# Neighbourhood attention: exponentials copied by a DMA into tiles of the rounded type, and transposed as that type

## The chip, the cores and the metric

The kernel runs on one core of a Trainium2 chip. The metric is the device time of one execution in microseconds (us), as the median of several runs; before the change it is 2466.07 us, from three runs between 2465.53 and 2466.47. PE is the matrix engine, PEld its weight loads, DVE the vector engine, ACT the scalar engine, POOL the third elementwise engine, and SP the engine that issues the kernel's DMAs.

## The reference

One layer of an encoder is applied to two sequences of 2048 tokens with 1024 columns each, all in 32-bit floats. Two attentions run beside each other on one input projection, and their outputs go into one product:

```python
def encoder_layer(x, p, ...):
    h = rms_norm(x, norm_w)
    proj = h @ w_in                       # 3328 columns
    q_a, k_a, v_a, g_a, q_b, k_b, v_b, g_b = jnp.split(proj, IN_SPLITS, axis=-1)
    ...
    o_a = windowed_gqa_sink(q_a, k_a, v_a, sink_a) * jax.nn.silu(g_a)
    ...
    o_b = neighbourhood_attn(q_b, k_b, v_b, rpb_b) * jax.nn.silu(g_b)
    x = x + jnp.concatenate([o_a, o_b], axis=-1) @ w_out
    gate = jax.nn.sigmoid(x @ w_ple_gate)
    return x + (p @ w_ple) * gate
```

The change is in the second attention, `neighbourhood_attn`. The tokens lie on a grid of 32 rows and 64 columns; each of 8 heads (64 columns a head) looks from a token at a window of 8 rows and 16 columns of the grid:

```python
sc = jnp.einsum('bnqhd,banchd->bnhqac', qr, kb) * scale
sc = jnp.where(mask, sc + bias, -jnp.inf)
pr = jax.nn.softmax(sc, axis=-1)
o = jnp.einsum('bnhqac,banchd->bnqhd', pr, vb)
```

## The kernel before

**Precision.** A matrix product is taken in `F32R`, a 32-bit type that PE multiplies with fewer bits than `F32`. To keep the accuracy, an operand is split into two `F32R` parts: high, the value as rounded when it is written as `F32R`, and low, the remainder. A product then takes three matmuls (high with high, low with high, high with low), or two where one side is laid out so that both of its parts stand beside each other. The parts are made by ACT (high) and DVE or POOL (low). Transposes were made in `F32` by PE: `tr` (L254) with the tile to be turned and an identity, `ident` (L111) or `rowwise` (L114), an identity with its columns in another order.

**Stages.** Up to about 804 us stage A works on the first attention, 32 blocks of tokens in two units each. From 804 to 1813 us stage B works on the second attention: 64 units `unit_b` (L845), one for a block of 8 x 16 queries and four of the eight heads. Then come the output product and the last product with its gate (from L1122 on). The products of a unit stand between those of a stream of projections (`proj_b`, L758, writing `pqk` and `pvg`) and later of `p @ w_ple` (`ple_ahead`), so that PE has products to do while the other engines work on the unit.

**One unit of stage B.** For each of four heads: `sc` makes the scores in `scb` (two matmuls), and `softmax` (L264) on DVE adds the bias and takes the maximum into a tile `s` (tag `s`, 5 buffers). After the fourth head `exps` (L275) makes the negated maxima `nm`, and ACT makes four exponentials, each in place in `s` (L284), and their sums. They are written in the order of heads 0, 2, 1, 3, and only the first is held in the program's order (`P`, L286). Then `load_values` (L862) loads the values in chunks, `vw`, three or four loads of up to 256 KB each (L870). For each head in that same order, `pt` turns three or four chunks of the exponentials (some 96 to 128 columns each) with `rowwise` into `ptb` (L255), ACT writes the high part and DVE the low part into `p_t`, and `po` multiplies them with `vw` into `pob`. `fin` scales with the gate and stores the block with a DMA to `ob_d` (L928).

**What sets the order.** `PLAN_B` (L94) gives the share of the unit's length at which each of these steps is written: scores from 0.00 to 0.11, exponentials and value loads at 0.16, the four groups of transposes at 0.45, 0.52, 0.60 and 0.74, with the steps named by `now` = 0 belonging to the unit before. Every matmul and transpose is pinned behind the one before it (`pinned`, L237), so PE's order is that of the program. On the other engines a scheduler orders the instructions by when it holds them to be ready, but for those under `P` or `behind`. SP issues all the DMAs that matter here, in one order, and waits with an instruction until all that it needs is done; what stands behind it waits too.

**The start.** `make_identity` and the copy to `rowwise` are POOL's. The first loads on SP are those of the first tokens (`stx`) with slices of the weights (`ws`, L232), then the second tokens, more weights (`ws`, `wg`) and small tables (`rw`, `snk_all`). The first products `pk` (keys and values of the first two blocks of tokens) and `pq` wait for them.

**Tiles by tag.** `ev` has 3 buffers: in stage A it holds pairs of score tiles (`s2`), in stage B from `ple_ahead` on the evictions `ev`. In between, in stage B, it has no other use.

Of the kernel before, what the change touches and what calls it, by code (L numbers as in the profile page):

```python
# [11 lines left out]
F32 = mybir.dt.float32  # L12
F32R = mybir.dt.float32r
# [55 lines left out]
SB = 5  # L69
# [11 lines left out]
TAIL = 8100  # L81
HOLD = {"wa": 20, "wb": 12, "wp": 0}
TW = 512
NU = SEQ // TW
AHEAD = 5
CP = 2
# [14 lines left out]
def emit(ctx, tc, io):  # L101
    nc = tc.nc
    dram = ctx.enter_context(tc.tile_pool(name="dram", bufs=1, space=bass.MemoryType.DRAM))
    cp = ctx.enter_context(tc.tile_pool(name="const", bufs=1))
# [3 lines left out]
        tag = PSM.get(tag, tag)  # L108
        return pp.tile(shape, F32, tag=tag, name=name, bufs=PSB[tag])

    ident = cp.tile([128, 128], F32, tag="ident", name="ident")  # L111
    make_identity(nc, ident)

    rowwise = cp.tile([128, 128], F32, tag="rowwise", name="rowwise")  # L114
    nc.gpsimd.tensor_copy(rowwise.rearrange("p (r c) -> p r c", c=16), ident.rearrange("p (c r) -> p r c", r=8))
    nw = cp.tile([128, KT], F32, tag="nw", name="nw")
    nc.scalar.dma_start(nw, io["norm_w"])
    ms_a = cp.tile([128, 2 * NT], F32, tag="ms_a", name="ms_a")
# [8 lines left out]
    main = ctx.enter_context(tc.tile_pool(name="main", bufs=1))  # L127
# [109 lines left out]
    def pinned(ins):  # L237

        if last_pe:
            tc.add_manual_dep(ins.ins, last_pe.pop().name,  # L240
                              mybir.DependencyInfo(mybir.DependencyClass.NoSync, mybir.DependencyReason.DATA),
                              reason="tensor engine order")
        last_pe.append(ins.ins)

    def behind(ins, other=None):

        tc.add_manual_dep(ins.ins, (other or last_pe[-1]).name,
                          mybir.DependencyInfo(mybir.DependencyClass.NoSync, mybir.DependencyReason.DATA),
                          reason="behind the product")
# [2 lines left out]
        pinned(nc.tensor.matmul(out, lhsT, rhs, start=start, stop=stop))  # L252

    def tr(out, in_, eye=ident):  # L254
        pinned(nc.tensor.transpose(out, in_, eye))  # L255

    def project(ps, xr, w, cost):

# [16 lines left out]
    def exps(sm, fct, gs, sink=None):  # L275

        mx, nm, den, rd, ss = (sm[k] for k in ("mx", "nm", "den", "rd", "s"))
        if sink is None:
            nc.vector.tensor_scalar_mul(nm, mx, -1.0)  # L279
            yield  # L280
        else:
            nc.vector.scalar_tensor_tensor(out=nm, in0=mx, scalar=-1.0, in1=sink[1], op0=ALU.mult, op1=ALU.min)
        for n_, i in enumerate((0, 2, 1, 3) if sink is None else range(4)):
            ex = nc.scalar.activation(ss[i], ss[i], AF.Exp, bias=nm[:, i:i + 1], accum_out=den[:, i:i + 1])  # L284
            if sink is None and n_ == 0:
                P(ex)  # L286
        if sink is not None:
            es = ap.tile([128, 4], F32, tag="es", name="es", bufs=3)
            nc.vector.tensor_tensor(out=es, in0=sink[0], in1=nm, op=ALU.add)
            nc.scalar.activation(es, es, AF.Exp)  # L290
            yield
            behind(nc.vector.tensor_tensor(out=den, in0=den, in1=es, op=ALU.add))
            nc.vector.reciprocal(out=nm, in_=den)
            nc.gpsimd.tensor_copy(rd, nm)
            nc.gpsimd.tensor_copy(rd[0:64, 1::2], nm[64:128, 0::2])
            nc.gpsimd.tensor_copy(rd[64:128, 0::2], nm[0:64, 1::2])
        else:
            nc.vector.reciprocal(out=rd, in_=den)
        nc.gpsimd.tensor_scalar_mul(rd, rd, fct)
        g2 = ap.tile([128, 4, HD], F32, tag="g2", name="g2", bufs=2)  # L300
        nc.gpsimd.tensor_tensor(out=g2, in0=gs.rearrange("p (h d) -> p h d", h=4),
                                in1=rd.unsqueeze(2).broadcast_to([128, 4, HD]), op=ALU.mult)
        sm["g2"] = g2.rearrange("p h d -> p (h d)")
        yield
# [14 lines left out]
    ap = ab_stack.enter_context(tc.tile_pool(name="ab", bufs=1))  # L319
# [138 lines left out]
    for i in range(2):  # L458
        t = ap.tile([128, 2, 512], F32R, tag=f"q2{i}", name=f"q2{i}")
# [204 lines left out]
    def unit_a(f, kv):  # L664
# [6 lines left out]
        def sc(i):  # L671
            pair, half = divmod(i, 2)
            a, z = span[half]
            c0, n = 128 * t - 128 + 64 * half, z - a
            if half == 0:
                pairs.append(ap.tile([128, 640], F32, tag="ev", name="s2", bufs=3))
                if not right:
                    nc.gpsimd.memset(pairs[pair][:, 256:320], 0.0)
            ps = ptile([128, 512], "sc", "sc")
            for j, q in enumerate(qs[f]):  # L680
                mm(ps[:, :n], q[kv][:, 128 * i:128 * i + 128], ks_a[:, kv, c0 + a:c0 + z], j == 0, j == 1)
            softmax(i, ps, n, mask[:, a:z], sm, pairs[pair][:, 320 * half + a:320 * half + z])
            if i == 3:
                got["ex"] = exps(sm, y[:, 11:12], gs[:, 256 * kv:256 * kv + 256],
                                 (snk[:, 0, 4 * kv:4 * kv + 4], snk[:, 1, 4 * kv:4 * kv + 4]))
                next(got["ex"])
# [158 lines left out]
    def unit_b(f):  # L845
# [34 lines left out]
        def sc(h):  # L880
            ps = ptile([128, 512], "sc", "scb")
            for j, q in enumerate(qs[f]):
                mm(ps[:, :n].rearrange("p (r c) -> p r c", c=ncol), q[h % 2][:, 128 * (h // 2):128 * (h // 2) + 128],
                   ks_b[h % 2][:, r0:r0 + nr, h // 2, c0:c0 + ncol], j == 0, j == 1)
            softmax(h, ps, n, bias[:, h, :n], sm)
            if h == 3:
                got["ex"] = exps(sm, hr_b[:, st:st + 1], gs)
                next(got["ex"])
# [43 lines left out]

    tiles = [(s, u) for s in range(2) for u in range(NU)]
    x1_d = [dram.tile([128, KT, TW], F32, tag=f"x1_d{n}", name=f"x1_d{n}") for n in range(len(tiles))]
    ple_d = [dram.tile([128, KT, TW], F32, tag=f"ple_d{n}", name=f"ple_d{n}") for n in range(len(tiles))]
    p_st, p_rs, early = {}, {}, {}

    def load_p(n):
        if n < len(tiles):
            s, u = tiles[n]  # L940
            p_st[n] = []
            for k in range(2):
                st = main.tile([128, TW], F32, tag="stage", name="p32", bufs=2)
                nc.sync.dma_start(st, io["p_t"][s][128 * k:128 * k + 128, TW * u:TW * u + TW])
                p_st[n].append(st)

    def split_p(n, later=False):

        t = p_rs[n] = main.tile([128, 2, 2, TW], F32R, tag="xr", name="p_r", bufs=2)

# [171 lines left out]
    with tc.tile_pool(name="c", bufs=1, reuse_waits="tile") as op:  # L1122
# [113 lines left out]
        for n, (stage, g) in enumerate(groups):  # L1236
            for h, t in ((0, 0), (1, 0), (1, 1), (0, 1)) if stage == 0 else ((0, 0), (1, 1), (1, 0), (0, 1)):
                for mi in range(4):
                    src = io["x_r"] if stage == 0 else x1_d
# [91 lines left out]
        for m in range(7 * len(groups)):  # L1331
            n, i = divmod(m, 7)
# [94 lines left out]
```

## Time and profile before

The profiled execution has a span of 2462.8 us, 3.3 us below the median of the runs.

| stretch (us) | length | PE busy | DVE busy | ACT busy | DMA share | GB/s |
|---|---|---|---|---|---|---|
| 400 to 800, stage A | 400 | 397.10 | 291.65 | 264.18 | 0.36 | 118 |
| 800 to 1000, stage B | 200 | 200.00 | 131.87 | 121.14 | 0.58 | 181 |
| 1200 to 1815, stage B | 615 | 614.00 | 408.19 | 392.26 | 0.68 | 218 |
| 1815 to 1900, between | 85 | 84.82 | 46.56 | 35.85 | 0.80 | 274 |
| 1900 to 2400, last products | 500 | 500.00 | 344.02 | 171.31 | 0.62 | 205 |

A row is a stretch of the span; the busy columns are the microseconds in which the engine worked, DMA share is the mean busy share of the core's 16 DMA engines, and GB/s is what they moved. The granted clock of PE is 1.00 in every stretch. In the profile an instruction is named by its line, its engine, and out<-in by the names of the tiles; `s<-s,nm` is an exponential, `ptb<-rowwise,s` a transpose of one.

### The profile page before, as it was taken

The numbers are of one execution on the slowest core, as the hardware profiler recorded it, in microseconds if no ns is written. First come the engines' busy times: TensorE is split into PE (matmuls) and PEld (weight loads), VectorE is DVE, ScalarE is ACT, GpSimd is POOL, SyncE is SP. The second block draws the span as 40 slices with busy tenths as digits, with TensorE's granted clock in tenths as the row PEclk, the third lists the DMA queues.
The fourth block names the chain that finished last, engine by engine and source line by source line (L and its number), as shares of the span: only waits on it lengthen the run. The fifth ranks groups of instructions, "written<-read, shape, count | busy, mean of one in ns | idle before, by whom it ended". The sixth has DMA issues, their size and how long they took to land.

```text
span 2462.8 us, 40532 instructions
## 1 busy us (share of the span) xinstructions
PE 2451.7 (100%) x13062; PEld 2075.4 (84%) x13062; DVE 1704.7 (69%) x4214; ACT 1413.1 (57%) x3408; POOL 856.8 (35%) x1363
## 2 busy tenths in 40 slices
PE   9999999999999999999999999999999999999999
PEld 8888888888888888888888888888888888888887
DVE  7777777777765666666666666666537655677776
ACT  6777776777664665656655566665763222344433
POOL 4555555555543544454444444443100000000000
PEclk9999999999999999999999999999999999999999
DMA  6332223332255565556955566667977445856765
GB/s 228 123 103 93 95 89 103 95 101 88 95 180 166 167 192 182 183 163 195 314 187 183 170 219 202 193 199 242 317 248 262 154 165 178 270 180 206 251 222 171
DMA packets 243316, 442.01 MB, mean 179 GB/s; under 512 B 27904, under 2 KB 82592, under 8 KB 237856
## 3 DMA queue, kind: packets, MB, share of 16 engines
q1 hardware_dynamic: 242816, 439.42, 54.8%
q8 instruction: 104, 1.70, 0.3%
q14 instruction: 108, 0.88, 0.1%
q10 hardware_dynamic: 288, 0.01, 0.0%
HBM read 309.29 MB, written 134.23 MB: 180 GB/s over the span
## 4 chain that ended last, share of the span: by engine, by line
PE 94%; DVE 2%; ACT 2%; POOL 1%; issue 1%; DMA 1%; SPq 0%; ACTq 0%; POOLq 0%; DVEq 0%
PE pvg L252 15%; PE pqk L252 14%; PE acca L1230 14%; PE accc L1230 11%; PE pg L252 6%; PE pq L252 6%; PE scb L252 4%; PE ptb L255 4%; PE pple L252 4%; PE pob L252 3%; PE po L252 3%; PE pk L252 3%; PE sc L252 3%; PE pt L255 2%; DVE pr L712 1%
## 5 line engine op out<-in xcount | busy, mean ns | idle before, releaser
L284 ACT ACTIVATE s<-s,nm 128x320 f32<-128x320 f32 (+6 forms) x512 | 294.5, 576 | 318.5 <-DVE nm L279 198.9
L252 PE MATMUL pvg<-wb,xr 128*128 128x512 f32 x1536 | 461.5, 407 | 0.0
L252 PE MATMUL pqk<-wa,xr 128*128 128x512 f32 x1536 | 442.9, 411 | 0.0
L252 PEld LDWEIGHTS pqk<-wa,xr 128*128 128x128 f32 x1536 | 266.1, 189 | 36.7
L252 PEld LDWEIGHTS pvg<-wb,xr 128*128 128x128 f32 x1536 | 266.8, 189 | 30.8
L1212 ACT CAST opd<-raw 128x512 fp32r<-128x512 f32 x224 | 131.5, 618 | 271.7 <-PE acca L1230 118.0
L353 POOL TENSOR_TENSOR xr<-stx,xr 128x512 fp32r<-128x512 f32 x186 | 238.9, 1295 | 101.3 <-ACT xr L352 76.8
L1213 DVE TENSOR_TENSOR opd<-raw,opd 128x512 fp32r<-128x512 f32 x224 | 146.7, 687 | 146.9 <-ACT opd L1212 146.9
L252 PE MATMUL pg<-wb,xr 128*128 128x512 f32 x768 | 233.3, 410 | 1.0 <-DVE vv L510 1.0
L252 PE MATMUL pq<-wa,xr 128*128 128x512 f32 x768 | 219.3, 400 | 0.0
L268 DVE CUSTOM_DVE_ANT_0 s<-scb,bias 128x288 f32<-128x288 f32 (+3 forms) x256 | 142.2, 556 | 104.6 <-PE scb L252 101.7
L137 POOL TENSOR_TENSOR yb<-vrb,power 128x8 f32<-128x8 f32 x64 | 106.4, 1662 | 222.1 <-DVE vrb L784 202.4
L1230 PE MATMUL accc<-opd,wb 128*128 128x512 f32 x768 | 176.7, 389 | 0.0
L1230 PE MATMUL acca<-opd,wa 128*128 128x512 f32 (+1 forms) x780 | 175.9, 386 | 0.5 <-ACT r L1308 0.5
L1230 PE MATMUL acca<-opd,s 128*128 128x512 f32 x768 | 175.4, 389 | 0.0
L1230 PEld LDWEIGHTS acca<-opd,wa 128*128 128x128 f32 x780 | 145.0, 188 | 30.2 <-ACT r L1308 0.7
L1230 PEld LDWEIGHTS acca<-opd,s 128*128 128x128 f32 x768 | 144.2, 188 | 29.9
L1230 PEld LDWEIGHTS accc<-opd,wb 128*128 128x128 f32 x768 | 144.2, 188 | 29.9
L919 DVE TENSOR_TENSOR otb<-pob,otb 64x512 f32<-64x512 f32 x128 | 88.1, 688 | 113.2 <-ACT otb L918 111.5
L252 PEld LDWEIGHTS pob<-p_t,vw 128*128 128x128 f32 (+2 forms) x832 | 132.6, 189 | 23.4 <-DVE p_t L900 3.4
L252 PEld LDWEIGHTS pq<-wa,xr 128*128 128x128 f32 x768 | 135.2, 189 | 17.3
L712 DVE TENSOR_TENSOR pr<-pt,pr 128x512 fp32r<-128x512 f32 (+2 forms) x248 | 135.4, 549 | 15.9 <-ACT pr L710 12.5
(171 smaller groups left out, 5169.9 us busy)
## 6 DMA issues: line engine op xcount, KB each, us to landing
stx<-x_b SPq DMA_DIRECT2D x128, 256.0 KB
vw<-v_d SPq DMA_DIRECT2D x112, 256.0 KB
stx<-x_a SPq DMA_DIRECT2D x64, 256.0 KB
stn<-x_n SPq DMA_DIRECT2D x64, 256.0 KB
v_d<-vb SPq DMA_DIRECT2D x64, 256.0 KB
ple_d<-ev SPq DMA_DIRECT2D x64, 256.0 KB
xres<-x_r SPq DMA_DIRECT2D x64, 256.0 KB
x_d<-r SPq DMA_DIRECT2D x64, 256.0 KB
```

Source lines behind the costliest of these rows:

```text
L137: nc.gpsimd.tensor_tensor(out=y, in0=v, in1=power.broadcast_to([128, n]), op=ALU.pow)
L252: pinned(nc.tensor.matmul(out, lhsT, rhs, start=start, stop=stop))
L255: pinned(nc.tensor.transpose(out, in_, eye))
L268: nc.vector.tensor_tensor_reduce(out=s, in0=ps[:, :n], in1=bias, scale=1.0, scalar=-3.0e38, op0=ALU.add, op1=ALU.max, accum_out=sm["mx"][: ...
L284: ex = nc.scalar.activation(ss[i], ss[i], AF.Exp, bias=nm[:, i:i + 1], accum_out=den[:, i:i + 1])
L353: low.tensor_tensor(out=lo, in0=raw, in1=hi.bitcast(F32), op=ALU.subtract)
L712: nc.vector.tensor_tensor(out=pr[r, 1, to], in0=pt[r, c], in1=pr[r, 0, to].bitcast(F32), op=ALU.subtract)
L919: nc.vector.tensor_tensor(out=ot[a:a + 64], in0=pq[a:a + 64], in1=ot[a:a + 64], op=ALU.add)
L1212: P(nc.scalar.copy(hi, v))
L1213: P(nc.vector.tensor_tensor(out=lo, in0=v, in1=hi.bitcast(F32), op=ALU.subtract))
L1230: pinned(nc.tensor.matmul(ps[:, cols], w[k][:, a, c:c + 128], o[:, b, cols], start=i in (0, 1, 4) and k == 0 and j == 0, stop=k == 3 and j ...
```

## The change

The two identities become `F32R` tiles. They are written from an `F32` identity in a tile `eye` of a temporary pool, which is closed at once, so that later tiles may lie on its place; `ident` is now written by DVE, `rowwise` by POOL as before. `tr` looks at the type of its input: an `F32R` tile is transposed as `F32R` into the same PSUM tile, with the `F32R` identity; any other tile as before, with the identity taken as `F32`. The new function `turned` takes a tile of the rounded type (name `tn`; for stage B of tag `ev`, one of its 3 buffers) and fills it by a DMA on SP from the given tile, read and written as `F32`, so the bits stay what they were. In `exps` every exponential of stage B is replaced by such a copy (`MOVE_B`), 256 in all; those of stage A are not (`MOVE_A`).

```diff
+MOVE_A, MOVE_B = False, True
...
-    ident = cp.tile([128, 128], F32, tag="ident", name="ident")
-    make_identity(nc, ident)
-
-    rowwise = cp.tile([128, 128], F32, tag="rowwise", name="rowwise")
-    nc.gpsimd.tensor_copy(rowwise.rearrange("p (r c) -> p r c", c=16), ident.rearrange("p (c r) -> p r c", r=8))
+    ident, rowwise = (cp.tile([128, 128], F32R, tag=n, name=n) for n in ("ident", "rowwise"))
+    with tc.tile_pool(name="eye", bufs=1) as ep:
+        eye_ = ep.tile([128, 128], F32, tag="eye", name="eye")
+        make_identity(nc, eye_)
+        nc.vector.tensor_copy(ident, eye_)
+        nc.gpsimd.tensor_copy(rowwise.rearrange("p (r c) -> p r c", c=16), eye_.rearrange("p (c r) -> p r c", r=8))
...
     def tr(out, in_, eye=ident):
-        pinned(nc.tensor.transpose(out, in_, eye))
+        if in_.dtype == F32R:
+            pinned(nc.tensor.transpose(out.bitcast(F32R), in_, eye))
+        else:
+            pinned(nc.tensor.transpose(out, in_, eye.bitcast(F32)))
+
+    def turned(src, tag, bufs):
+
+        t = (ap if tag == "ev" else main).tile([128, 512], F32R, tag=tag, name="tn", bufs=bufs)[:, :src.shape[-1]]
+        nc.sync.dma_start(t.bitcast(F32), src)
+        return t
...
                 P(ex)
+            if sink is None and MOVE_B:
+                ss[i] = turned(ss[i], "ev", 3)
+            elif sink is not None and MOVE_A:
+                ss[i] = turned(ss[i], "s", SB)
```

Lines of the changed kernel: the copy stands on L265, the exponential on L295 (before L284), the value loads on L885 (L870), the store to `ob_d` on L943 (L928). In the pieces of order below a name carries the number of its buffer, and the square brackets hold what the instruction waits for: `Activation`, `PE`, `DVE` and `Pool` are engines, `DMAHW` the lanes of the DMA queue.

On SP, in one unit of stage B, these instructions stood in a row before:

```order
L870 DMA vw_13603<-v_d002_300 128x512 [waits DMAHW7_49,PE_49]
L870 DMA vw_13415<-v_d001_299 128x512 [waits DMAHW0_49,PE_49]
L870 DMA vw_13601<-v_d002_300 128x512 [waits DMAHW1_49,PE_49]
L928 DMA ob_d0_85<-o_tb_13424 128x2x128 [waits DMAHW2_49,DVE_49]
L817 DMA v_d012_304<-vb_13466 8x8x512 [waits DMAHW3_49,DVE_49]
L817 DMA v_d013_305<-vb_13466 16x8x512 [waits DMAHW4_49]
L620 DMA sums0_236<-raw_12891 128x2048 [waits DMAHW5_49,Pool_49]
L335 DMA stx_13562<-x_b 128x512 [waits DMAHW6_49,Pool_49]
L335 DMA stx_13585<-x_b 128x512 [waits DMAHW7_49,Pool_49]
```

With the change, SP has at the same place of the program:

```order
L885 DMA vw_13729<-v_d002_306 128x512 [waits DMAHW3_49,PE_49]
L885 DMA vw_13533<-v_d001_305 128x512 [waits DMAHW4_49,PE_49]
L885 DMA vw_13727<-v_d002_306 128x512 [waits DMAHW5_49,PE_49]
L265 DMA tn_13514<-s_13468 128x384 [waits DMAHW6_49,Activation_49]
L265 DMA tn_13517<-s_13488 128x384 [waits DMAHW7_49]
L265 DMA tn_13520<-s_13476 128x384 [waits DMAHW0_49,Activation_49]
L943 DMA ob_d0_91<-o_tb_13542 128x2x128 [waits DMAHW1_49,DVE_49]
L265 DMA tn_13523<-s_13499 128x384 [waits DMAHW2_49,DMAHW6_49,PE_49,Activation_49]
L832 DMA v_d012_310<-vb_13584 8x8x512 [waits DMAHW3_49,DVE_49]
L832 DMA v_d013_311<-vb_13584 16x8x512 [waits DMAHW4_49]
L635 DMA sums0_242<-raw_12985 128x2048 [waits DMAHW5_49,Pool_49]
L350 DMA stx_13680<-x_b 128x512 [waits Pool_49]
```

Three copies stand between the value loads and the store to `ob_d`, in the order of heads 0, 2, 1, and the fourth (head 3) behind that store; it takes the buffer of the first copy, and so waits for PE as well.

On ACT the order of the exponentials in that unit is the same before and after; with the change it reads:

```order
L295 ACTIVATE s_13488,den_13463<-s_13488,nm_13462 128x384 [waits DMAHW0_49,DVE_49]
L933 COPY otb_13418<-pob_13491 64x512 [waits PE_49]
L295 ACTIVATE s_13468,den_13463<-s_13468,nm_13462 128x384 [waits DMAHW7_49]
L295 ACTIVATE s_13476,den_13463<-s_13476,nm_13462 128x384 [waits DMAHW7_49]
L295 ACTIVATE s_13499,den_13463<-s_13499,nm_13462 128x384 [waits DMAHW1_49]
```

The first to run is that of head 2 (`s_13488`), the second that of head 0 (`s_13468`), whose copy stands first on SP and whose transposes stand first on PE. On PE the order is the same row for row, with `tn` for `s` as the source of 832 transposes.

At the start, SP began before with the tokens and the weights in turn:

```order
L335 DMA stx_123<-x_a 128x512
L232 DMA ws_121<-w_in 128x2x256
L335 DMA stx_126<-x_a 128x512
L232 DMA ws_121<-w_in 128x2x256
L232 DMA ws_122<-w_in 128x2x256 x2
L335 DMA stx_131<-x_a 128x512 [waits DMAHW0_49]
L335 DMA stx_133<-x_a 128x512 [waits DMAHW1_49]
```

With the change, SP begins with:

```order
L234 DMA ws_143<-w_in 128x2x512 x2
L234 DMA wg_152<-w_in 128x512
L234 DMA wg_154<-w_in 128x512
L234 DMA wg_156<-w_in 128x512
L234 DMA wg_158<-w_in 128x512
L422 DMA rw_162<-rope_w 128x64 [waits DMAHW0_49]
L444 DMA snk_all_246<-sink 128x8 [waits DMAHW1_49]
L350 DMA stx_129<-x_a 128x512 [waits DMAHW2_49,DVE_49,Pool_49]
L234 DMA ws_127<-w_in 128x2x256 [waits DMAHW3_49]
L350 DMA stx_132<-x_a 128x512 [waits DMAHW4_49]
```

The first load of tokens now stands behind eight others, and waits for DVE and POOL, which read `eye`.

## The prediction

> **What bounds the kernel now.** I read the page's busy times and its chain first: they say which engine sets the end.
>
> ```profile
> span 2462.8 us, 40532 instructions
> PE 2451.7 (100%) x13062; PEld 2075.4 (84%) x13062; DVE 1704.7 (69%) x4214; ACT 1413.1 (57%) x3408; POOL 856.8 (35%) x1363
> ...
> PE 94%; DVE 2%; ACT 2%; POOL 1%; issue 1%; DMA 1%; SPq 0%; ACTq 0%; POOLq 0%; DVEq 0%
> ```
>
> PE has work for the whole span but 11 us, and the chain is PE's for 94%. So a microsecond in which PE waits is a microsecond of the total, and one that PE is spared is a microsecond gained. Next, stretches of stage B and of the last stage, with matmuls, clock and DMA share, and the instructions that write `ptb`:
>
> ```profile
> 1000.00:1200.00 200.00, 200.00 (x1094) 168.62 (x1093) 132.00 (x336) 120.75 (x285) 97.30 (x112) 1.00 0.62 196
> ...
> 1900.00:2400.00 500.00, 500.00 (x2207) 414.13 (x2207) 344.02 (x550) 171.31 (x305) 0.00 (x0) 1.00 0.62 205
> ...
> L255 PEld LDWEIGHTS ptb<-rowwise,s x832: 123/138/144, 804.2 to 1812.7; 128*128 128x128 f32 x90, 128*96 128x96 f32 x40, 128*120 128x120 f32 x37
> ```
>
> In stage B, 804 to 1813 us, PE has no gap, DMA is busy for 0.62 of the time, and 832 transposes stand in 256 groups, four groups a unit, 64 units. The last stage gives the price of a 512-wide product: 500 us ÷ 2207 = 0.2266 us.
>
> **The transposes themselves.** One unit's timeline on PE and ACT, from the first group of transposes on:
>
> ```profile
> 1015.77 0.49 PE L255 MATMUL ptb<-rowwise,s 128*128 128x128 f32 x3
> ...
> 1016.95 0.41 ACT L899 CAST p_t<-ptb 128x304 fp32r<-128x304 f32 x1
> ...
> 1017.27 1.18 PE L252 MATMUL pqk<-wa,xr 128*128 128x512 f32 x4
> 1018.29 0.49 PE L255 MATMUL ptb<-rowwise,s 128*128 128x128 f32 x3
> 1018.53 0.95 PE L252 MATMUL pqk<-wa,xr 128*128 128x512 f32 x3
> 1019.32 0.45 PE L252 MATMUL pob<-p_t,vw 128*128 128x256 f32 x3
> 1019.61 1.13 PE L252 MATMUL pqk<-wa,xr 128*128 128x512 f32 x4
> 1020.58 0.49 PE L255 MATMUL ptb<-rowwise,s 128*128 128x128 f32 x3
> 1020.83 0.95 PE L252 MATMUL pqk<-wa,xr 128*128 128x512 f32 x3
> ```
>
> Durations here overlap, so I take starts. From 1017.27 to 1018.53 lie four products and three transposes: 1.26 - 4 × 0.2266 = 0.354, or 0.118 us a transpose. From 1018.53 to 1020.83 lie seven products, three `pob` products and three transposes: 2.30 - 7 × 0.2266 - 0.354 = 0.360 for the three `pob`. The cast shows that such a group of `pob` moves 304 columns twice, high and low, so 608; at the rate of a 512-wide product that is 0.27 us. It takes 0.36. Short products of the rounded type thus cost 0.12 us each however few columns they move: something per product binds, and each brings new weights. That matters because the built program, in its instruction words, gives the 832 changed transposes the same mode bits as ordinary products of that type, on the weight load and on the matmul, while the other 1298 transposes keep the bits they had. So the nearest row is `pob`: 0.120 against 0.118, no change, **0 us**. Ends: the best case is the streaming rate, 128 ÷ 512 × 0.2266 = 0.057, which gives 832 × (0.057 - 0.118) = -51 us; the worst is 832 × 0.002 = +2.
>
> The Trainium skill, "TensorE: Matmul & The Clock Gate", section "Back-to-back issue gap", states a gap of N ÷ 2.4 + 2.5 ns, 56 ns for 128 columns, which by itself would make the change a gain of 52 us. Its section "LDWEIGHTS (loading the stationary operand)" puts a load of 128 columns at 128 ÷ 1.2 = 107 ns, near the 0.12 us of the `pob` row; so the trace sides with the second here, and the sum would gain 9 us by it.
>
> **The copies.** The order on PE is the same row for row but for the name of the source; a copy stands now between an exponential and the transposes that PE meets in that fixed order. What counts is how long before its transposes an exponential is ready:
>
> ```profile
> 1012.31 0.62 ACT L284 ACTIVATE s<-s,nm 128x384 f32<-128x384 f32 x1 [3.37 <-DVE nm L279]
> ...
> 1013.05 0.58 ACT L918 COPY otb<-pob 64x512 f32<-64x512 f32 x1
> 1013.65 0.62 ACT L284 ACTIVATE s<-s,nm 128x384 f32<-128x384 f32 x1
> 1014.17 0.19 ACT L284 ACTIVATION_READ_ACCUMULATOR s<-s,nm 128x1 f32 x1
> ...
> 1012.07 1.28 SPq L870 DMA_DIRECT2D vw<-v_d  x3
> 1015.64 0.37 SPq L928 DMA_DIRECT2D ob_d<-o_tb  x1
> ```
>
> By the order on ACT the exponential at 1012.31 is that of the head transposed second; the head transposed first comes at 1013.65 and is done at 1014.36. That is so in 61 of the 64 units. Its transposes start at 1015.77, their weights some 0.23 us before (the first of all: 804.2): at 1015.54. The lead is **1.18 us**. Into it must go the issue on SP, the way through the queue and the landing. The DMA view of 1012 to 1018 us, in 40 bins of 0.15 us:
>
> ```profile
> DMA  0000000187589999997697654330005994000000
> GB/s 0 0 0 0 0 0 0 55 123 191 191 314 396 396 382 355 423 410 260 246 355 273 232 218 150 123 123 27 0 0 154 382 280 113 0 0 0 0 0 0
> ```
>
> The three loads of `vw`, issued from 1012.07, move bytes from 1013.05 to 1016.2. The store of `ob_d` (128 KB), alone, is issued at 1015.64 and moves from 1016.5 to 1017.1, its end 1.46 us after issue. In the new order the copies stand right behind those three `vw`. A copy here has 128 x 384 x 4 = 197 KB, 0.5 us at the view's 400 GB/s. Bounds for the first copy, issued at 1014.40:
> - alone in the queue, as `ob_d`: 1014.40 + 1.46 + 0.16 for the larger size = 1016.02, late by 0.5 us;
> - behind the `vw` bytes: 1016.2 + 0.5 = 1016.7, late by 1.15 us, without the way from the last byte to PE;
> - as the kernel's first load, whose 256 KB are issued at 0.72 and used at 3.74 (rows below), 3.0 us: 1017.42, late by 1.9 us.
>
> The middle of the last two, **1.5 us**, is my value, since loads stand ahead in most units: 64 × 1.5 = **96 us**, ends 32 and 122. Seven units have a longer lead, and mostly a longer queue ahead:
>
> ```profile
> 981.26 0.58 ACT L284 ACTIVATE s<-s,nm 128x360 f32<-128x360 f32 x1
> 981.74 0.19 ACT L284 ACTIVATION_READ_ACCUMULATOR s<-s,nm 128x1 f32 x1
> ...
> 984.28 0.49 PE L255 MATMUL ptb<-rowwise,s 128*120 128x128 f32 x3
> ```
>
> Here 984.05 - 981.93 = 2.1 us, with four loads ahead in place of three; I give them the same price. One stall a unit: once PE has waited for the first group, the second copy, about 0.5 us behind the first, has 1.26 us until its group. The fourth copy waits for a buffer, that is for the first transposes. Its own come 4.8 us after those (1020.58 against 1015.77), more than the 3.0 us of the slowest bound. Behind it SP holds two `v_d` stores, `sums` and two `stx`, which before were issued from 1018.77 on; it is released by about 1017.5. Without that cover, a late `xr` would stop PE. Bytes: 256 copies of 197 KB on average are 50 MB in 1009 us, a quarter more than the 196 GB/s there. `s` buffers come free sooner, which gives nothing, as PE waits for none.
>
> **The start.** The temporary `eye` makes the buffers laid over its place wait for it, and the scheduler moves other loads ahead: two `ws` (512 KB each) and four `wg` (256 KB each), 2.1 MB, now leave before the first tokens.
>
> ```profile
> 1.47 3.78 PE L252 MATMUL pwarm<-warm 128*128 128x512 f32 x8 [1.47 <-DVE warm L379]
> ...
> 0.72 0.39 SPq L335 DMA_DIRECT2D stx<-x_a  x1
> ...
> 3.74 0.62 ACT L352 CAST xr<-stx 128x512 fp32r<-128x512 f32 x1 [0.81 <-DMA stx<-x_a]
> ...
> 5.36 7.99 PE L252 MATMUL pk<-wx,xr 128*128 128x256 f32 x48
> ...
> 9.05 1.25 ACT L352 CAST xr<-stx 128x512 fp32r<-128x512 f32 x2
> ...
> 13.18 1.09 PE L252 MATMUL pq<-wa,xr 128*128 128x512 f32 x4
> ...
> GB/s 0 16 229 345 314 302 332 338 375 412 403 414 385 381 393 387 389 385 369 376 362 373 385 373 337 339 135 35 0 0 0 0 0 72 256 197 0 84 389 551
> ```
>
> The last row has bins of 1 us. Adding it up, 0.50 MB had moved at 3.74 and 2.27 MB at 9.05; with 2.1 MB ahead these amounts are reached at 9.9 and 14.4: 6.2 and 5.4 us later. The cast of the second tokens carries the end of the `pk` products and so the start of `pq`, 13.18: +5.4. PE stands from 5.25 to about 11.5, and the first row shows 0.47 us a product where 0.2266 is normal, so a slow first phase may come again; the 3.78 us of it would cost at most 1.9. I take 5.4 + 1.1 = **6.5 us**, ends 4.9 and 8. The cover that the start had, work already loaded, is gone; what was loaded early (`wg`) was not waited for.
>
> **Sum**, against the profiled execution: 2462.8 + 0 + 96 + 6.5 = 2565.3. The runs shown have a median of 2466.07, 3.3 us around the span, which I keep: **2568.6 us**.
>
> **Rivals.**
> - *The transposes gain and the copies still stall*: at the streaming rate, 2568.6 - 51 = 2518. For it: a matmul of 128 columns need not last longer than its columns. Against it: the `pob` row and the equal mode bits. Chance 0.10.
> - *The other side, faster*: the same gain, and the first copy usable within 1.18 us of its exponential, so that no group waits: 2466.07 - 51 + 6.5 = 2422. It decides at a lateness of 0.7 us a unit, where 64 × 0.7 = 44.5 eats 51 - 6.5. Against it: `ob_d` alone needed 1.46 us to its last byte. Chance 0.03.
> - *The copies are hidden and the transposes cost what they did*: 2472 or, if the start is made good later, 2466. Same objection; chance 0.03, within 0.2%.
> - *The queue gets worse*: late `xr` or a lowered PE clock behind each stall, as in the first microseconds: beyond 2600. The granted clock is 1.00 throughout and no 3.78 us gap arises; chance 0.06.
> - My forecast has 0.78.
>
> **How the numbers follow.** With its unknowns the forecast covers 2466 + 4.9 + 32 = 2503 to 2466 + 8 + 122 + 2 = 2598, and the first rival lies inside; 2505 to 2600 leaves out some 0.15. A measurement of this kernel tells 0.2% (5 us) from no change. Faster: the second rival, 0.03. Same: the third, 0.03. Slower: the rest, 0.94.
>
> **What would show it.** PE idle before `ptb`, released by the DMA that writes `tn`, some 64 times with 0.5 to 1.9 us each and nearly always at a unit's first group; the three transposes between products still at 0.11 to 0.12 us; `pk` beginning near 11.5 and `pq` near 18.5; the last stage as long as before. I am wrong if no idle time stands before `ptb`, if the group shrinks to 0.06 us a transpose, or if the waiting goes to the second or fourth head.

## The result and the profile after

The changed kernel takes 2606.57 us (median of four runs, 2602.96 to 2613.68) against 2465.84 us before: a ratio of 1.0572, 95% interval 1.0555 to 1.0588. The prediction was 2568.6 us with a range up to 2600. The sign was right, the size was not: the loss is 140.7 us where 102.5 were forecast, and it lies outside the range.

The page of the profiled execution, with its busy times and the chain:

```profile
span 2606.8 us, 41312 instructions
PE 2469.0 (95%) x13062; PEld 2070.2 (79%) x13062; DVE 1710.0 (66%) x4215; ACT 1414.7 (54%) x3408; POOL 857.0 (33%) x1363
...
PE 76%; DMA 10%; ACT 6%; DVE 5%; issue 1%; POOL 1%; SPq 0%; ACTq 0%; POOLq 0%; DVEq 0%
```

PE is no longer busy for the whole span, and the chain now goes through DMA, ACT and DVE for a fifth of the time. What PE waited for, in total, how often, and the longest:

```profile
PE ptb L258 <- DMA tn<-s: 103.6, 70, 7.0
PE pk L254 <- issue: 7.7, 1, 7.7
PE ptb L258 <- DVE q L853: 6.3, 4, 1.6
PE ptb L258 <- DVE qg L807: 5.8, 4, 2.1
PE pob L254 <- DMA vw<-v_d: 2.1, 4, 1.2
```

Three rows stand before `ptb`: 78 waits with 115.7 us. By the trace these are the first groups of all 64 units, 106.3 us, and the fourth groups of 14 units, 9.4 us; the second row is the start. The instructions that write `ptb` (count, shortest, median and longest duration in ns, first and last start), and the whole of stage B as a window, first of the changed kernel and then of the kernel before (length, then busy time of PE, PEld, DVE, ACT and POOL, clock, DMA share, GB/s):

```profile
L258 PEld LDWEIGHTS ptb<-rowwise,tn x832: 122/138/224, 813.8 to 1956.3; 128*128 128x128 f32 x90, 128*96 128x96 f32 x40, 128*120 128x120 f32 x37
```

```profile
813.80:1956.90 1143.10, 1025.44 (x5507) 841.64 (x5508) 674.27 (x1689) 631.05 (x1478) 441.86 (x516) 0.98 0.70 226
```

```profile
804.20:1813.30 1009.10, 1008.66 (x5509) 848.31 (x5509) 668.90 (x1691) 629.94 (x1479) 442.42 (x520) 1.00 0.65 206
```

Stage B begins 9.6 us later and is 134.0 us longer; what follows it takes as long as before (2606.8 - 1956.3 = 650.5, and 2462.8 - 1812.7 = 650.1). So the loss is the start and stage B, as forecast. In B, PE is idle for 117.7 us where it was idle for 0.4; but its busy time also grew by 16.8 us, and the granted clock is 0.98 where it was 1.00.

One unit, with the rows of SP, ACT and PE that carry the wait (start, duration, engine, line):

```profile
1063.20 1.27 SPq L885 DMA_DIRECT2D vw<-v_d  x3
...
1064.74 0.62 ACT L295 ACTIVATE s<-s,nm 128x384 f32<-128x384 f32 x1
...
1065.47 1.81 SPq L265 DMA_DIRECT2D tn<-s  x3
...
1065.66 1.39 PE L254 MATMUL pvg<-wb,xr 128*128 128x512 f32 x5
...
1067.80 0.42 PE L258 MATMUL ptb<-rowwise,tn 128*128 128x128 f32 x3 [0.75 <-DMA tn<-s]
...
1068.63 0.47 SPq L265 DMA_DIRECT2D tn<-s  x1
...
1073.25 0.42 PE L258 MATMUL ptb<-rowwise,tn 128*128 128x128 f32 x3 [0.61 <-DMA tn<-s]
```

The exponential that is needed first is again the second on ACT. Its copy is issued at 1065.47, and the transposes start at 1067.80, 2.33 us later. The wait is longer than the 0.75 us that the row gives: five products from 1065.66 need 5 x 0.2266 us, so the next could have begun at 1066.79, while the profile counts PE as busy until 1067.05. About 0.26 us of this wait is thus booked as busy time. The last two rows show a second wait: the fourth copy is issued at 1068.63, once the first transposes have freed its buffer, and its group stands until 1073.25.

### The profile page after: what moved, and what is told of

It reads as the page before. It is cut to its first block, busy times and chain, and to the rows that moved or that the text cites. A ratio compares the mean times of both kernels' runs of the same rounds, so it can differ in the third digit from the quotient of the medians.

```text
span 2606.8 us, 41312 instructions
## 1 busy us (share of the span) xinstructions
PE 2469.0 (95%) x13062; PEld 2070.2 (79%) x13062; DVE 1710.0 (66%) x4215; ACT 1414.7 (54%) x3408; POOL 857.0 (33%) x1363
## 4 chain that ended last, share of the span: by engine, by line
PE 76%; DMA 10%; ACT 6%; DVE 5%; issue 1%; POOL 1%; SPq 0%; ACTq 0%; POOLq 0%; DVEq 0%
PE acca L1245 13%; PE pqk L254 12%; PE accc L1245 10%; DMA tn<-s 9%; PE pg L254 6%; PE pq L254 6%; PE pvg L254 6%; ACT s L295 4%; PE scb L254 3%; PE pk L254 3%; PE po L254 3%; PE ptb L258 3%; PE sc L254 3%; PE pple L254 2%; PE pob L254 2%; PE pt L260 2%
## 5 line engine op out<-in xcount | busy, mean ns | idle before, releaser
L295 ACT ACTIVATE s<-s,nm 128x320 f32<-128x320 f32 (+6 forms) x512 | 294.4, 576 | 319.1 <-DVE nm L290 199.2
L254 PE MATMUL pqk<-wa,xr 128*128 128x512 f32 x1536 | 449.0, 415 | 0.0
L258 PEld LDWEIGHTS ptb<-rowwise,tn 128*128 128x128 f32 (+2 forms) x832 | 94.3, 140 | 170.6 <-DVE q L853 78.7
L258 PE MATMUL ptb<-rowwise,tn 128*128 128x128 f32 (+2 forms) x832 | 105.1, 242 | 115.7 <-DMA tn<-s 103.6
L915 DVE TENSOR_TENSOR p_t<-ptb,p_t 128x368 fp32r<-128x368 f32 (+5 forms) x256 | 121.2, 488 | 110.3 <-ACT p_t L914 105.5
L914 ACT CAST p_t<-ptb 128x368 fp32r<-128x368 f32 (+5 forms) x256 | 104.5, 427 | 117.4 <-PE ptb L258 115.4
```

The lines of the kernel that those rows point to most:

```text
L258: pinned(nc.tensor.transpose(out.bitcast(F32R), in_, eye))
L914: nc.scalar.copy(hi, pf)
L915: nc.vector.tensor_tensor(out=lo, in0=pf, in1=hi.bitcast(F32), op=ALU.subtract)
```

## The experiments

The runs stand in five groups. Each kernel was timed against the kernel before on the same chip; the median of that lay between 2465.4 and 2466.9 us.

### The start

`eye_only` has no copies:

```diff
-MOVE_A, MOVE_B = False, True
+MOVE_A, MOVE_B = False, False
```

> No copies and F32 transposes as before; only the two identities of the rounded type and the temporary eye stay. If the start alone is what it was in the changed kernel (first pk products 7.7 us late, nothing made good later): 2465.8 + 7.5 to 9 = 2473 to 2475. By the prediction's term: +6.5, 2472. If the late start is made good later: 2466.

2476.09 us against 2466.92, ratio 1.0035 (1.0022 to 1.0048): +9.2 us. The start costs what it looked like in the trace, 2.7 us more than the prediction's 6.5, and nothing of it is made good later. `start_back` is the changed kernel with its copies; it takes the temporary pool away and keeps the rest:

```diff
-    with tc.tile_pool(name="eye", bufs=1) as ep:
-        eye_ = ep.tile([128, 128], F32, tag="eye", name="eye")
...
     ap = ab_stack.enter_context(tc.tile_pool(name="ab", bufs=1))
+    eye_ = ap.tile([128, 128], F32, tag="o_t", name="eye", bufs=2)
+    make_identity(nc, eye_)
```

> The changed kernel with eye in a buffer that stage B alone uses (o_t), so that SP begins with the tokens again. If the start and the copies add up: 2606.6 - 8 = 2598, with the first pk products back at 5.4 us and the waits at the transposes unchanged. If the start's delay hides part of the later waits: 2606.

2604.96 us (2599.07 to 2608.64). PE's rows at its start are back where they were:

```profile
1.47 3.62 PE L249 MATMUL pwarm<-warm 128*128 128x512 f32 x8 [1.47 <-DVE warm L393]
5.21 1.43 PE L249 MATMUL pk<-wx,xr 128*128 128x256 f32 x6
```

So the start is repaired by a buffer that is not reused early. The time fell by 1.6 us only and not by 8, and runs of these two kernels lie 10 us apart, so the medians do not show that start and copies add up. The two traces show more: stage B begins 7.5 us earlier and ends 5.5 us earlier than in the changed kernel, and the clock of PE was halved in it for 54.6 us in place of 44.4 (the third group is on the clock). Why the runs differ so much was not settled.

### The transposes

`plain` keeps the copies and turns the copied bits as `F32`:

```diff
-tr(pt[:kc, c:c + 128], sm["s"][h][:, kc * j:kc * j + kc], rowwise)
+tr(pt[:kc, c:c + 128], sm["s"][h][:, kc * j:kc * j + kc].bitcast(F32), rowwise)
```

> The changed kernel with its copies, but the copied tiles are transposed as F32 (same bits, same identity read as F32). By the prediction's term the transposes cost the same: 2606. By the trace's groups they are longer by 0.05 to 0.08 us a group: 2606 + 16 = 2622.

2621.27 us, 14.7 more than the changed kernel. The transposes did get shorter. In the changed kernel's unit above:

```profile
1069.24 1.16 PE L254 MATMUL pqk<-wa,xr 128*128 128x512 f32 x4
1070.24 0.37 PE L258 MATMUL ptb<-rowwise,tn 128*128 128x128 f32 x3
1070.44 0.93 PE L254 MATMUL pqk<-wa,xr 128*128 128x512 f32 x3
```

From 1069.24 to 1070.44 lie four products and three transposes, as in the prediction's reading of the kernel before: 1.20 - 4 x 0.2266 = 0.294 us, or 0.098 a transpose in place of 0.118. Times 832 that is 16.6 us. `rounded` has these transposes without any copy, and the start of `start_back`. It leaves out the low part of the exponentials, which ACT now rounds as it writes them, but not the time of making that part:

```diff
-            ex = nc.scalar.activation(ss[i], ss[i], AF.Exp, bias=nm[:, i:i + 1], accum_out=den[:, i:i + 1])
+            to = ss[i] if sink is not None else \
+                ap.tile([128, 512], F32R, tag="ev", name="tn", bufs=3)[:, :ss[i].shape[-1]]
+            ex = nc.scalar.activation(to, ss[i], AF.Exp, bias=nm[:, i:i + 1], accum_out=den[:, i:i + 1])
+            ss[i] = to
```

> start_back without copies: ACT writes the exponentials of stage B straight into the tiles of the rounded type, which drops their low bits (the low part of the probabilities is then zero, the time of making it stays). It has the new transposes and no wait for a DMA. By the prediction's term (a transpose costs 0.12 us either way): 2466 within 3. If the new transposes are shorter, as the groups in the changed kernel's trace look (0.05 to 0.08 us less a group): 2450, 16 us less. At the streaming rate in full: 2466 - 51 = 2415.

2468.31 us, ratio 1.0005 (0.9995 to 1.0014): no gain. PE's busy time fell by 10 us (2441.7 against 2451.7), but new waits stand beside it:

```profile
PE pob L249 <- DVE p_t L917: 7.4, 15, 0.8
PE pple L249 <- ACT ev L1025: 4.8, 5, 1.8
```

The fourth exponential here waits on ACT for the buffer of the first, with everything behind it on ACT. That this is the cause of the two rows was not tried. This run left open whether the gain can be had end to end; the last group answers it.

### The clock

Windows of the changed kernel around two of the longer waits, each with the 3.41 us ahead of it (length, then PE, PEld, DVE, ACT, POOL busy, clock, DMA share, GB/s):

```profile
1224.94:1228.35 3.41, 1.46 (x8) 0.89 (x6) 2.19 (x7) 1.67 (x6) 2.21 (x5) 1.00 0.95 279
1228.35:1235.17 6.82, 5.98 (x21) 4.83 (x22) 3.79 (x8) 4.16 (x9) 1.50 (x2) 0.50 0.90 295
...
1863.24:1866.65 3.41, 0.00 (x0) 0.00 (x0) 1.55 (x4) 1.44 (x4) 1.69 (x4) 1.00 1.00 360
1866.65:1873.47 6.82, 3.83 (x15) 3.07 (x16) 0.76 (x2) 2.01 (x4) 0.00 (x0) 0.50 0.82 267
```

After PE had stood for 1.95 and for 3.41 of 3.41 us, its clock is at half for the next 6.82. There are ten stretches of halved clock in this execution, of 3.41 or 6.82 us, 44.4 us together. `filled` gives PE something to do while it waits:

```diff
             pt = ptile([128, 512], "pt", "ptb")
+            for _ in range(6 if x == 0 else 0):
+                mm(pt.rearrange("p (r c) -> p r c", c=64), rowwise, ks_b[0][:, r0:r0 + 8, 0, :], True, True)
```

> The changed kernel with six extra 512-wide products (6 x 0.2266 = 1.36 us) on PE ahead of the first transposes of each unit, written into the tile that the transposes then overwrite. They fit into a wait of 1.85 us on average. If the halved clock follows PE's idle time of about 2 us and more: no or few halved stretches, 2606.6 - 17 to 20 + about 3 in the units with a shorter wait = 2590. If the clock falls for another reason, or the extra products only add: 2606 to 2625 with the stretches still there.

The profiled execution has one halved stretch inside stage B in place of ten, and a clock of 0.999. The same 1153 us of both kernels, first the changed one, then this:

```profile
804.00:1957.00 1153.00, 1034.08 (x5550) 848.64 (x5549) 678.83 (x1704) 634.76 (x1490) 446.23 (x522) 0.98 0.70 226
```

```profile
804.00:1957.00 1153.00, 1106.97 (x5943) 909.54 (x5942) 681.97 (x1707) 636.30 (x1493) 449.17 (x523) 1.00 0.70 226
```

384 extra products are 384 x 0.2266 = 87.0 us of work, yet PE's busy time grew by 72.9 only: the other work became some 14 us shorter with the clock back. That is the price of the halved clock, and it came with the idle time and went with it. The size is rough, as fewer waits are booked as busy here too; in the changed kernel's own trace the steps between matmuls that are no waits grew by 12 us inside the ten stretches, which is near it. The total missed its mark of 2590: the span is 2607.7 us, because the fill was longer than many waits (73 us of idle time for 87 us of products), and the median is 2617.33 us, with spans of 2607.7, 2614.4, 2616.6 and 2624.0 us at clocks of 0.999, 0.997, 0.995 and 0.992. Why the clock fell in those other executions can't be seen, as only the first has a trace; in these four the time follows the clock.

### The wait

`order` lets ACT make the exponential of head 0 first:

```diff
-            if sink is None and n_ == 0:
-                P(ex)
+            if sink is None and n_ > 0:
+                behind(ex, exs[-1])
+            exs.append(ex.ins)
```

> ACT makes the exponential of the head that is transposed first before the others (about 1.3 us earlier in most units); the three others follow as they did. If the copy's own way (2.7 us from issue to PE) sets the wait: the first wait falls from 1.85 us to 0.3 to 0.5 us a unit and the second group waits about as much, 64 x 0.5 = 32 us in place of 118, the clock stays at 1.00: about 2490 to 2500. If the bytes of the value loads ahead in the queue set it, the copy lands when they have gone by, however early it is issued: a wait of 1.1 us stays, 64 x 1.1 = 70 us: 2540.

2550.98 us, 55.6 less than the changed kernel; the waits before `ptb` fell from 115.7 to 63.8 us:

```profile
PE ptb L258 <- DMA tn<-s: 56.6, 45, 4.8
...
PE ptb L258 <- DVE q L855: 5.3, 6, 1.8
...
PE ptb L258 <- DVE qg L809: 1.2, 1, 1.2
...
PE ptb L258 <- DVE rd L315: 0.7, 2, 0.5
```

So the lead of the exponential is what decides, but 1.3 us more of it bought 0.8 us a unit, and the time stayed above both values expected. The copy, issued earlier, took longer: where PE waited for a unit's first copy, it came 3.6 us after its issue (median of 56 units), and 2.9 us in the changed kernel (64 units). `values_behind` and `order_values` put the value loads of a unit behind its first copy on SP, the first alone and the second with `order`:

```diff
-                nc.sync.dma_start(v[:kc]..., v_d[half, s, cb]...)
+                behind(nc.sync.dma_start(v[:kc]..., v_d[half, s, cb]...), copied_at[-4])
```

> On SP the value loads of a unit stand behind its first copies; the exponentials keep their order on ACT. If the value loads ahead in the queue lengthen the copy's way: from 2.7 to about 1.9 us, a wait of 0.8 to 1.1 us a unit left, 50 to 70 us, with fewer halved stretches: 2515 to 2545. If they don't: as the changed kernel, 2600. If the values then come late for the product with them: a new wait before pob, and no gain.

> Both edits. If the exponential's place and the queue add up: first copy issued 0.75 us after the first exponential's start and landed by 2.7, its transposes due at 3.3; second landed by 4.0, due at 4.5: hardly a wait left, the shorter transposes (16 us) stand against the late start (9 us): 2460 to 2470. If the late values hold up pob instead, some 0.5 us a unit: 2490 to 2500.

Both lose: 2686.12 and 2661.09 us. In `values_behind`, PE's waits are:

```profile
PE ptb L258 <- DMA tn<-s: 83.5, 59, 6.5
PE pob L254 <- DMA vw<-v_d: 59.6, 79, 1.9
...
PE ptb L258 <- DVE qg L809: 7.1, 5, 1.8
```

Before `ptb` 25 us went (115.7 to 90.6), and 59.6 us before `pob` took their place: the values are late now. The clock is lower too, 0.983 against 0.991. A unit of this kernel shows what a copy takes when nothing of its unit is ahead of it:

```profile
985.26 1.81 SPq L265 DMA_DIRECT2D tn<-s  x3
...
987.72 0.51 PE L258 MATMUL ptb<-rowwise,tn 128*128 128x128 f32 x4 [1.22 <-DMA tn<-s]
```

From issue to PE 2.46 us, for 256 KB. With loads ahead the unit above took 2.33 us, at 192 KB, and the median of the 64 units is 2.9 us in the changed kernel and 2.7 here. So the queue is the smaller part in most units, and the way itself the larger. The Trainium skill, "DMA: Bandwidth & Descriptors", section "Anatomy of one DMA — SWDGE (gpsimd) path", gives about 2.0 us fixed and the bytes at 436 GB/s for another way of issuing, 2.6 us for this size as an estimate; the row is close to it.

`act_queue` is `order` with three of four copies issued by ACT, on a queue of its own:

```diff
-ss[i] = turned(ss[i], "ev", 3)
+ss[i] = turned(ss[i], "ev", 3, nc.scalar if n_ < 3 else nc.sync)
```

> The kernel order with the first three copies of a unit issued by ACT on its own queue, right behind their exponentials; SP's queue of loads is no longer ahead of them. If the loads ahead in SP's queue make up what is left of the waits (63 us): first wait near zero, 2551 - 50 = 2500, less what ACT loses by issuing (192 x 0.1 to 0.6 us on an engine that is not the bound). If the copy's own way or the shared DMA engines set it: 2540 to 2551.

2735.19 us, the slowest of all, with the clock at 0.958. A unit, by its issue on SP, its issue on ACT, and PE:

```profile
997.98 1.28 SPq L887 DMA_DIRECT2D vw<-v_d  x3
...
999.19 0.47 ACTq L265 DMA_DIRECT2D tn<-s  x1
...
1003.59 0.50 PE L258 MATMUL ptb<-rowwise,tn 128*128 128x128 f32 x4 [1.73 <-DMA tn<-s]
```

4.40 us from issue to PE (the median of the 64 units is 5.1 us), though the copy did not stand behind the loads in SP's queue. The DMA view shows them ahead all the same, first from the issue to 1001.00, then from there to 1002.00 (q1 is SP's queue, q10 ACT's; packets, MB, share of the 16 engines):

```profile
q1 hardware_dynamic: 299, 0.55, 88.5%
```

```profile
q1 hardware_dynamic: 104, 0.18, 55.5%
q10 hardware_dynamic: 88, 0.18, 45.7%
```

For 1.8 us after its issue the copy moved nothing while the value loads moved. Over the 64 units, the more SP's queue moved after the issue, the later the copy's first bytes came: 1.1 us after it at the least, 2.1 us in the median. So a queue of its own did not get the copy past the loads. Why it was slower than behind them on SP's queue stays open.

`fourth` puts the fourth copy into a tile of tag `s`, of which one is free by then:

```diff
-ss[i] = turned(ss[i], "ev", 3)
+ss[i] = turned(ss[i], *(("ev", 3) if n_ < 3 else ("s", SB)))
```

> The changed kernel with the fourth copy of a unit written into a tile of tag s (free sooner now) in place of the buffer of the first copy, so that it no longer waits for the first transposes, and SP no longer stands behind them. If the wait at the fourth group comes from that buffer: its 10 to 12 us go, and nothing else: 2595. If SP's standing there also made the first copies late (bias and value loads issued later): more, 2570 to 2590. If the fourth copy, now earlier in the queue, only shifts traffic: 2606.

2592.91 us, 13.7 less than the changed kernel, and 104.5 us of waits before `ptb` (94.0, 5.5 and 5.0) in place of 115.7. No fourth group waits any more, so the second wait of 14 units was the buffer's.

### Can the copies be hidden?

`later` joins `order`, `fourth` and `start_back`, and writes the four groups later:

```diff
-    (0.45, 1, "pt", 0), (0.52, 1, "pt", 1), (0.60, 1, "pt", 2), (0.66, 1, "po", 0), (0.74, 1, "pt", 3), (0.80, 1, "po", 1),
+    (0.53, 1, "pt", 0), (0.60, 1, "pt", 1), (0.68, 1, "pt", 2), (0.74, 1, "po", 0), (0.82, 1, "pt", 3), (0.88, 1, "po", 1),
```

> Four edits that should let the transposes' gain through: the first head's exponential first on ACT, the fourth copy in tag s, eye in o_t, and the four groups of transposes with the products behind them 0.08 of a unit (1.25 us) later in PE's order. Lead of the first copy 1.18 + 1.3 + 1.25 = 3.7 us against the 2.5 to 4.2 us that a copy took from issue to PE: waits in the units with a bias load or long queue only, 64 x 0.1 to 0.4 us; with 16 us of shorter transposes: 2466 - 16 + 6 to 26 = 2456 to 2476. If the queue grows with the earlier fourth copy: 2490.

2532.36 us, above all that was expected. The copies are nearly hidden, but another wait took their place:

```profile
PE pob L249 <- DVE p_t L916: 32.1, 40, 1.5
PE ptb L253 <- DMA tn<-s: 18.0, 12, 3.9
```

The parts `p_t` now come late for `pob`. So the order on PE has to stay, and the exponentials have to come earlier. `early` does that: each head's maximum is negated by itself. It keeps the start of `start_back` and the fourth copy's tile of `fourth`.

```diff
+    def exp_b(sm, *heads):
+        mx, nm, den, ss = (sm[k] for k in ("mx", "nm", "den", "s"))
+        for i in heads:
+            nc.vector.tensor_scalar_mul(nm[:, i:i + 1], mx[:, i:i + 1], -1.0)
+        for i in heads:
+            ex = nc.scalar.activation(ss[i], ss[i], AF.Exp, bias=nm[:, i:i + 1], accum_out=den[:, i:i + 1])
...
+            ss[i] = turned(ss[i], *(("s", SB) if i == 3 else ("ev", 3)))
...
             softmax(h, ps, n, bias[:, h, :n], sm)
+            if h != 1:
+                exp_b(sm, *{0: (0,), 2: (2,), 3: (1, 3)}[h])
```

> eye in o_t, the fourth copy in tag s, and each head's negated maximum and exponential as soon as its own scores are there (head 0 after the first pair of score products, head 2 after the third, 1 and 3 after the fourth), in place of all four after the last. PE's order is that of the changed kernel. The first exponential then comes some 2.5 to 3 us earlier than in the changed kernel (1.7 us from the scores, 1.3 us from ACT's order): its copy has 4 us where 2.5 to 4.2 were needed. If the copies' lateness was all that stood against the shorter transposes: waits of 0 to 0.3 us a unit, 2466 - 16 + 0 to 20 = 2450 to 2470. If the copies' bytes also delay values, tokens or the high and low parts behind them: new waits before pob or pqk, 2480 to 2500.

2475.47 us: 131 of the 140.7 us are gone, some 9 of them by the start, with all 256 copies in place. That is 5 us above the range expected. PE's only notable wait for them is 8.8 us, in 8 places:

```profile
PE ptb L253 <- DMA tn<-s: 8.8, 8, 3.1
```

`early_none` is its control, without copies; `early_skip` leaves them out in nine units, in which PE of `early`, matmul by matmul against the kernel before, lost 18 us together:

```diff
+            if copy:
+                ss[i] = turned(ss[i], *(("s", SB) if i == 3 else ("ev", 3)))
...
+                exp_b(sm, f - 2 * NT not in (25, 26, 57, 58, 59, 60, 61, 62, 63), *{0: (0,), 2: (2,), 3: (1, 3)}[h])
```

> early without any copies: exponentials early, transposes as F32 from the score tiles, as before the change. Control for early. If the early exponentials themselves cost or gain nothing: 2466 within 2, and the 9 us by which early is slower are the copies' doing. If the early exponentials collide with other work of ACT in the last units: up to 2475.

> early with copies and shorter transposes in 55 units; nine units (the two during which the second half's weights are loaded, and the last seven, beside the first loads of the next stage) transpose as F32 without a copy. In early PE gained about 0.25 us in each undisturbed unit and lost some 18 us in those nine. If the transposes' gain is real and the copies' loss sits only in those nine: 2466 - 55 x 0.25 = 2452 to 2456. If what was lost there is not the copies' (early_none then shows it too): 2466 to 2472. If the gain is given back elsewhere: 2466 and over.

`early_none` takes 2466.31 us, ratio 1.0001 (0.9992 to 1.0010): the early exponentials alone do nothing. `early_skip` takes 2458.05 us against 2466.18, ratio 0.9969 (0.9959 to 0.9980): 8.1 us faster than the kernel before, 2 us short of what was expected. The end of stage B in two windows, first of `early`, then of `early_skip`:

```profile
1690.00:1815.00 125.00, 115.90 (x607) 94.88 (x606) 71.31 (x200) 79.34 (x183) 23.06 (x39) 0.95 0.91 306
```

```profile
1690.00:1815.00 125.00, 121.89 (x669) 101.89 (x669) 75.60 (x209) 85.85 (x197) 25.03 (x42) 1.00 0.82 286
```

With copies, the DMA engines are busy for 0.91 there, PE is idle for 9 us of 125, and the clock is at 0.95; without them it issues 62 matmuls more in the same time. So the transposes' gain is real end to end, and what `early` still lost came with the copies that stood beside the loads of the next weights and of the next stage, in waits and in halved clock.

## Why the prediction was wrong

Its steps one by one, by the trace of the changed kernel and the runs:

| step | predicted (us) | measured (us) | from |
|---|---|---|---|
| start | 6.5 | 9.2 | `eye_only` |
| waits for the copies | 96 | 128.4 | starts of the groups that waited, against the kernel before |
| transposes | 0 | -14.7, or -16.6 | `plain`, or the rows between products |
| clock | 0 | 14 | `filled` |
| sum | 102.5 | 137, with -14.7 | |

PE's order is the same in both kernels, so the traces can be compared matmul by matmul. A wait is here what the step from the product before it to the group's first transpose grew by, so it holds the part that is booked as busy. The loss is 140.7 us; some 4 us of it are assigned to no step, of which 2 are PE's idle time elsewhere in stage B. That the two terms put at nothing nearly cancel is luck.

**The bound and the mechanism** were right: PE has work for the whole span, so each wait shows in the total; the waits stand before `ptb`, once a unit in 50 of the 64, released by the copy; the exponential needed first comes second on ACT. `order` and `early` show that its lead decides.

**The step that failed first** is the sentence "The granted clock is 1.00 throughout and no 3.78 us gap arises", with which the rival of a lowered clock was put at 0.06. That rival, beyond 2600 us, is the one that came; without the 14 us of the clock the time would have been 2593. A gap of 1.9 us was enough to halve the clock, and one of 7.0 us arose. The Trainium skill, "TensorE: Matmul & The Clock Gate", section "HAM oscillation — how this bites in real kernels", puts the limit at idle gaps of about 3.4 us; the windows above show the halved clock after 1.95 us, so the measurement is stricter than the rule.

**The waits were under-sized**, though not in the usual unit: there the price of 1.5 us was right. In 52 units the first group came 1.50 us late on average, 78.0 us together. So close a hit is luck, as the price was the middle of two bounds. First, the prediction gave the units with four value loads ahead "the same price": these seven, the one at 984.28 of its rows among them, came 2.7 us late, 18.6 us together. Second, units beside other loads had no price of their own: five, beside loads of weights or of the next stage, came 2.8 to 7.2 us late, 20.1 us together. The latest is this, where `ple_d`, `wb` and `p` go ahead of the copies. Third, "One stall a unit" left out the fourth copy: the 4.8 us that its group comes behind the first were held against 3.0 us for a copy, and the trace shows 1068.63 to 1073.25, 4.6 us from an issue that itself had to wait for the first transposes; 14 units, 11.7 us (`fourth`: 13.7 us).

```profile
1858.82 0.93 SPq L959 DMA_DIRECT2D p<-p_t  x2
1859.80 0.49 SPq L992 DMA_DIRECT2D wb<-sp_oa  x1
1860.38 0.65 SPq L1001 DMA_DIRECT2D ple_d<-ev  x1
1861.09 0.67 SPq L885 DMA_DIRECT2D vw<-v_d  x1
1862.47 6.19 SPq L265 DMA_DIRECT2D tn<-s  x3
```

```profile
1869.63 0.72 PE L258 MATMUL ptb<-rowwise,tn 128*128 128x128 f32 x4 [7.03 <-DMA tn<-s]
```

The lower bound, "alone in the queue, as `ob_d`" with 1.62 us, was none for this copy either: with nothing of its unit ahead, one of 256 KB took 2.46 us to PE. The 1.46 us of `ob_d` ended at its last byte and not at PE.

**The transposes** were put at no change, by the `pob` row. The two prices at the two ends, -51 and +2, held the truth at -16.6; the nearest row was the wrong choice. A row of three now lasts 0.37 us in place of 0.49, but the next product starts only 0.04 us sooner after the group's start (1070.24 to 1070.44, before 1018.29 to 1018.53). By the starts in the trace of `early_skip`, one transpose of a group follows the other after 0.061 to 0.064 us (0.109 before), while the product behind the group comes 0.06 to 0.08 us after the last (0.03 before); so a third of the -51 remains. It also shows that the prediction's reading of `pob`, 0.12 us for a short product "however few columns" it moves, does not hold for these. That the weights of the product behind hold it up would fit; it wasn't tried.

**The rivals.** "The transposes gain and the copies still stall" was right in both halves, though the gain was a third of its 51 us. The faster side needed the copy within 1.18 us of its exponential, and that did not come about. With more lead `early_skip` reaches that side: there 5.1 us lie between an exponential's end and its transposes in the median unit, 3.7 more than before the change.

## What to carry to other kernels

When a copy by a DMA is put between a producer and an engine that never waits, measure first how long the producer is ready ahead of its consumer, and hold some 3 us against it, and more where loads stand ahead in any queue; then move the producer, not the consumer or the other loads. Count an idle PE twice: once as time, once as the clock that it may lose where half of a 3.41 us stretch is idle. A gain on the bounding engine of 0.02 us an instruction counts only where nothing in its supply becomes later, and can be taken in most units while the crowded ones are left as they were.

## What the runs showed of the hardware

- The granted clock of PE falls to 0.50 in pieces of 3.41 us or twice that. In the changed kernel the 3.41 us ahead of each of the ten held 1.75 us of idle time or more. The length of a wait alone does not decide: of fifteen waits of 1.9 us or more, five halved nothing, among them one of 3.31 us from 1885.29, which fell across two such stretches with 1.8 and 1.5 us. The limit is not sharp, as that 1.8 shows; in `values_behind` and `order_values` halved clock also followed 1.3 to 1.7 us.

```profile
1883.70:1887.11 3.41, 1.59 (x8) 0.93 (x7) 1.68 (x4) 2.82 (x9) 1.21 (x3) 1.00 0.86 323
1887.11:1890.52 3.41, 1.92 (x12) 1.65 (x13) 0.95 (x2) 1.20 (x3) 1.21 (x3) 1.00 0.69 240
```

- A transpose of the rounded type costs 0.098 us between 512-wide products, one in `F32` 0.118, at the same 128 x 128 elements.
- A copy of 256 KB was slower from ACT's queue, 4.40 us to PE, than from SP's with the value loads behind it, 2.46 us; while SP's queue moved its loads, the one on ACT's moved nothing for 1.8 us after its issue.
